# Delta rule: powers, weight casts and value scaling placed elsewhere in ScalarE's queue, the weight subtraction placed later, one output transpose in another PSUM bank

## The chip, the core and the metric

The kernel runs on one core of a Trainium2 chip. The core has five engines that work side by side, each through its own queue in order: TensorE (PE, matrix products; PEld is its weight load), VectorE (DVE), ScalarE (ACT), GpSimd (POOL) and SyncE (SP), which issues most of the DMA transfers. They wait for one another through semaphores. Working data lies in the on-chip memory SBUF; matrix products land in PSUM, which has eight banks. The metric is the device time of one execution in microseconds, lower is better.

## The reference

One inference step of a two-layer encoder over 2048 prompt tokens and 32 sample tokens. The first layer is a gated delta rule with 8 heads of width 128, the second a sliding-window attention. The part that matters here:

```python
def step(s, xs):
    qd, kd, ui, wi, ai, gl = xs
    v_new = ui - jnp.einsum('bhck,bhkv->bhcv', wi, s)
    o = jnp.einsum('bhck,bhkv->bhcv', qd, s) + jnp.einsum('bhij,bhjv->bhiv', ai, v_new)
    s = s * gl[..., None, None] + jnp.einsum('bhck,bhcv->bhkv', kd, v_new)
    return s, o
```

with, for each chunk, decays `exp(gcum_i - gcum_j)`, powers `exp(gcum)`, a unit lower triangular inverse, and afterwards

```python
o = o * lax.rsqrt(jnp.mean(o * o, -1, keepdims=True) + RMS_EPS) * norm_w * jax.nn.silu(z)
out = o.reshape(b, l, A_VW) @ w_out
```

The gate `z` is a slice of `x @ w_in`; the kernel forms such products from a high and a low part of each operand, so a weight is first cast to its high part (`w_hi`), and the low part (`w_lo`) is the weight less that.

## The kernel before

The program has three stages. First come the projections with the short convolution. Then comes the delta stage, which this change touches: `Delta.run` goes over 17 chunks (one of the 32 sample tokens, 16 of 128 prompt tokens). Last come the output projection and the second layer. In the delta stage the orders of TensorE, VectorE and ScalarE are those in which the code emits their instructions, written out by hand; GpSimd's and the DMA queue's orders are the scheduler's.

Each pass of the loop works on several chunks at once: `ch` (chunk i) is finished, `nx` (i+1) gets its errors and the last part of its inverse, `n2` (i+2) is prepared, `n3` (i+3) gets loads and decays. A step is a generator, and `go(...)` runs each generator named up to its next `yield`. The steps, with their lines before the change:

- `lower` (L538): products k·k (`g`), times the decays `E` on VectorE (`npr`, L550), copies to `nb` on ScalarE (L554), a transposition to `L` on VectorE (L559).
- `chain` (L562): the inverse of 32-row blocks, `tm` and `Tt` (L572, L575). For `n2` its first 25 columns run on GpSimd over nearly a whole pass, the rest on VectorE in the next pass.
- `spread` (L638): two VectorE transpositions `tcp` (L645, L646), then ScalarE spreads them (L651). `invert` (L653): products `bps` (L669, L675, L682, L688, L693) with ScalarE copies between them; the last (L694) writes `u`, which `changes` needs.
- `changes` (L707): products `vp` of `u` and `vn` (L714), copied to `vs` by ScalarE (L716). `seen` (L720): the output products `op` (L728, L732). `advance` (L737): products `sp` (L744) and the new state on VectorE (L750). `errors` (L697): products `ks` (L703), subtracted from `vn` (L704).
- `turn_k` (L578): transposes k and scales it on ScalarE to `kd`. `turn_v` (L592): transposes v (`vtr`, L599) and scales it to `vn`: the first four heads in one VectorE operation (L601), the last four in four ScalarE operations (L604).
- `powers` (L623): two ScalarE exponentials of `gb`, in place (L627). `fade` (L630): k and q times `gb` on VectorE (L635). `decays` (L524): one VectorE operation and eight ScalarE exponentials for `E` (L534).
- `squares`, `norms`, `scale`: the output's root mean square, on ScalarE (L760) and VectorE (L767, L423 to L434, L776). `emit` (L779): four transposes of the output into a PSUM tile (`otr`, L786), times z on VectorE (L787), stored.

PSUM: pool `pa` (tag `tr`) and pool `pc` (tag `sc`) have two banks each, `pb` and `pd` one. `vp`, `otr`, `sp` and `ks` take turns in `pc`; the 64-wide products of `invert` alternate between `pb` and `pa`.

Up to pass 10 `fill(us)` puts gate products of the first layer between the steps (`late_z`, L274; `project` with L77 to L79). Their weights are fetched ahead into `w_raw`, cast by ScalarE (L53) and subtracted by VectorE (L54), both in `split`, which `side(False)` calls in the middle of a pass, after the squares. Such a cast falls on every second pass. In the last passes, and afterwards, output products take the filler's place (L1076 to L1078).

Of the kernel before, what the change touches and what calls it, by code (L numbers as in the profile page):

```python
# [10 lines left out]
F32 = mybir.dt.float32  # L11
F32R = mybir.dt.float32r
I32 = mybir.dt.int32
AF = mybir.ActivationFunctionType
ALU = mybir.AluOpType
# [80 lines left out]
class P1:  # L96
# [166 lines left out]
    def split(self):  # L263
        if self.fetched is not None:
            self.next = split_fetched(self.nc, self.wp, self.fetched, self.sub)
            self.fetched = None

# [182 lines left out]
class Delta:  # L450
# [141 lines left out]
    def turn_v(self, ch):  # L592
        nc, G, n = self.nc, self.G, ch.n
        ch.vn = []
        for q in range(2):
            vn = self.four.tile([128, 4, 128], F32, tag="vn", name="vn")
            tr = self.pa.tile([128, 4, 128], F32, tag="tr", name="vtr")
            for j in range(4):
                nc.tensor.transpose(tr[:n, j, :], ch.v[q][:, j, :n], G["ident"][:, :])  # L599
            if q == 0:  # L600
                nc.vector.tensor_tensor(out=vn[:n], in0=tr[:n], in1=self.bc(G["hn"][:n, ch.ti, 0:4], n), op=ALU.mult)  # L601
            else:
                for j in range(4):
                    nc.scalar.activation(vn[:n, j, :], tr[:n, j, :], AF.Copy, scale=G["hn"][:n, ch.ti, 4 + j:5 + j])  # L604
            ch.vn.append(vn)
# [173 lines left out]
    def emit(self, ch):  # L779

        nc, V, T, n = self.nc, self.nc.vector, self.T, ch.n
        for q in range(2):
            z = ch.z[q]
            tr = self.pc.tile([128, 4, 128], F32, tag="sc", name="otr")
            for j in range(4):
# [5 lines left out]
    def run(self, chunks, S, first, second, side, done):  # L791
# [44 lines left out]
        for i in range(len(chunks) + 1):  # L836
# [32 lines left out]
            go(a, t, a, t, seen, sq)  # L869
            side(False)  # L870
            fill(2 * more + gate)
# [10 lines left out]
            if i == 0:  # L882
# [4 lines left out]
                (self.norms, ch), (self.scale, ch)))  # L887
            go(e, t, t)
            drain(t)
            if nx:  # L890
                self.spread(nx)
            go(w, e)
            if n3:
# [3 lines left out]
            d = gen(self.decays, n3)  # L897
            p = gen(self.powers, n2)
            go(v)
            fill(gate)  # L900
            go(r, r, r, g, r, r, v, r, k, r, d)
            if i > self.OPEN:
# [8 lines left out]
            seen = gen(self.seen, nx)  # L911
            go(w, r, p, r, seen, k, r, d, r)
            if n3:
# [7 lines left out]
            fill(more)  # L921
            go(v, o, d)
            if i + 3 == len(chunks):
# [673 lines left out]
def program(tc, I, O, T, G):  # L1597
# [32 lines left out]
    def side(o):  # L1630
        if o is None:
            left.close()
            o1.append(O1(tc, left, I, O, T, G))
        elif o1 and o:
            next(o1[0].on.rest, None)
            if o1[0].steps == 8:
                o1[0].on.tabs = o1[0].on.tables()
            o1[0].steps += 1
        elif not o1 and not o:
            p1.split()  # L1640

    def outputs():
# [207 lines left out]
```

## Time and profile before

| | us |
|---|---|
| median of 3 runs | 2244.25 |
| lowest and highest | 2241.93 and 2248.31 |
| profiled execution | 2235.55 |
| span of the profiled execution | 2233.8 |

| share of the span | busy us | share |
|---|---|---|
| TensorE | 2161.8 | 97% |
| its weight loads | 1982.5 | 89% |
| VectorE | 1378.5 | 62% |
| ScalarE | 900.5 | 40% |
| GpSimd | 838.1 | 38% |

The profile describes one execution. A row of a timeline gives start, length, engine, line, operation, output and inputs, and in brackets how long the engine stood idle before it and which instruction released it. A row of waits gives the waiting engine and instruction, what it waited for, the total, the number of times and the longest. Lengths of matrix products include a tail in which the result drains while the next group already runs, so the distance of starts says more than the length. The share of a whole span is an average over stages: what an edit of one stage is worth is read in that stage.

### The profile page before, as it was taken

What the parts mean: (1) busy time and instruction counts of PE and PEld (TensorE: products, weight loads), DVE (VectorE), ACT (ScalarE), POOL (GpSimd) and SP (SyncE); (2) the same over time, 40 slices, a digit from 0 to 9 for tenths busy, and PEclk for the clock granted to TensorE, in tenths of its full rate; (3) what the DMA queues carried; (4) which work ended last, traced back from release to release, by engine and by line L of the source; (5) the groups of instructions that cost most, each with busy time, mean ns of one, the idle gap of its engine ahead of it and who ended that gap; (6) DMA issues with size and microseconds to landing.
All of it is one profiled execution on the core that took longest, in us unless ns stands there. A gap on an engine that the chain in (4) does not pass through costs nothing.

```text
span 2233.8 us, 36601 instructions
## 1 busy us (share of the span) xinstructions
PE 2161.8 (97%) x13706; PEld 1982.5 (89%) x13706; DVE 1378.5 (62%) x2713; ACT 900.5 (40%) x2235; POOL 838.1 (38%) x1189
## 2 busy tenths in 40 slices
PE   8999999999999999999989999999999999999997
PEld 6999999999999888898878788999999977778885
DVE  3676666753476687878867886135442235668774
ACT  4344444433333566667742212222112235445541
POOL 1422122221211477777731201046441214556563
PEclk9999999999999999999999999999999999999999
DMA  5222122333445244345526764365222277233311
GB/s 195 67 64 82 60 75 66 111 104 110 125 121 162 93 132 126 122 127 188 189 103 202 224 200 141 111 219 175 73 75 69 84 178 249 76 95 96 111 59 57
DMA packets 250529, 274.47 MB, mean 123 GB/s; under 512 B 76096, under 2 KB 195200, under 8 KB 250080
## 3 DMA queue, kind: packets, MB, share of 16 engines
q1 hardware_dynamic: 238352, 248.84, 36.3%
q10 hardware_dynamic: 12000, 23.30, 3.0%
q8 instruction: 108, 1.77, 0.3%
q14 instruction: 69, 0.57, 0.1%
HBM read 168.53 MB, written 103.92 MB: 122 GB/s over the span
## 4 chain that ended last, share of the span: by engine, by line
PE 83%; ACT 7%; DVE 4%; DMA 3%; POOL 1%; issue 1%; ACTq 0%; DVEq 0%; SPq 0%; POOLq 0%
PE ps L77 16%; PE ps L79 16%; PE ps L78 16%; PE po L1076 5%; PE po L1078 4%; PE po L1077 4%; PE ot L1567 4%; PE S L1546 2%; PE tr L1561 2%; PE vp L714 1%; DMA act_raw<-s_hT 1%; ACT kd L588 1%; PE op L732 1%; PE sp L744 1%; PE gq L618 1%
## 5 line engine op out<-in xcount | busy, mean ns | idle before, releaser
L77 PE MATMUL ps<-act_hi,w_hi 128*128 128x416 f32 x2000 | 707.0, 354 | 6.4 <-ACT w_hi L53 5.1
L79 PE MATMUL ps<-act_hi,w_lo 128*128 128x416 f32 x2000 | 704.9, 353 | 1.8 <-POOL w_lo L54 1.2
L78 PE MATMUL ps<-act_lo,w_hi 128*128 128x416 f32 x2000 | 701.6, 351 | 0.5 <-DVE act_lo L69 0.4
L77 PEld LDWEIGHTS ps<-act_hi,w_hi 128*128 128x128 f32 x2000 | 376.8, 189 | 11.9 <-ACT w_hi L53 6.1
L79 PEld LDWEIGHTS ps<-act_hi,w_lo 128*128 128x128 f32 x2000 | 376.1, 188 | 6.7 <-POOL w_lo L54 1.7
L78 PEld LDWEIGHTS ps<-act_lo,w_hi 128*128 128x128 f32 x2000 | 376.4, 188 | 5.4 <-DVE act_lo L69 1.1
L54 POOL TENSOR_TENSOR w_lo<-w_raw,w_hi 128x1024 fp32r<-128x1024 f32 x51 | 135.4, 2655 | 555.7 <-ACT w_hi L53 501.5
L196 DVE SCALAR_TENSOR_TENSOR y<-R,convw,y 128x2083 f32<-128x2083 f32 x72 | 173.7, 2414 | 109.7 <-ACT y L194 74.1
L572 POOL TENSOR_TENSOR tm<-L,Tt 128x60 f32<-128x60 f32 (+19 forms) x373 | 141.1, 378 | 119.6 <-DVE tm L572 47.5
L1554 POOL TENSOR_TENSOR P<-P,sm 128x384 f32<-128x384 f32 (+2 forms) x128 | 100.5, 807 | 181.7 <-DVE sm L1433 106.6
L575 POOL TENSOR_TENSOR Tt<-Tt,tm 128x60 f32<-128x60 f32 (+19 forms) x373 | 152.9, 410 | 29.2
L1429 ACT ACTIVATE P<-S,nm 128x192 f32<-128x192 f32 (+2 forms) x260 | 104.6, 418 | 93.3 <-DVE nm L1422 40.4
L227 ACT COPY R<-ps 128x416 f32<-128x416 f32 (+1 forms) x144 | 61.3, 449 | 199.0 <-PE ps L79 174.7
L53 ACT CAST w_hi<-w_raw 128x1024 fp32r<-128x1024 f32 x62 | 64.9, 1047 | 128.8 <-PE ps L78 99.4
L1076 PE MATMUL po<-wo_hi,g_hi 128*128 128x512 f32 x256 | 103.8, 406 | 1.8 <-ACT hT L1183 1.8
L1273 POOL TENSOR_TENSOR rs<-rs,sin 128x416 f32<-128x416 f32 x50 | 71.1, 1421 | 78.8 <-DVE rs L1272 72.1
L1078 PE MATMUL po<-wo_hi,g_lo 128*128 128x512 f32 x256 | 100.6, 393 | 0.0
L1567 PE MATMUL ot<-pt,vd 128*128 128x256 f32 x372 | 98.7, 392 | 1.9 <-ACT pt L1563 1.5
L1077 PE MATMUL po<-wo_lo,g_hi 128*128 128x512 f32 x256 | 100.3, 392 | 0.0
L1076 PE MATMUL po<-wo,g_hi 128*128 128x512 f32 x240 | 99.3, 414 | 0.0
L1078 PE MATMUL po<-wo,g_lo 128*128 128x512 f32 x240 | 96.2, 401 | 0.0
L1077 PE MATMUL po<-wo,g_hi 128*128 128x512 f32 x240 | 96.1, 400 | 0.0
(304 smaller groups left out, 3984.3 us busy)
## 6 DMA issues: line engine op xcount, KB each, us to landing
w_raw<-in_w_in SPq DMA_DIRECT2D x40, 512.0 KB
w_raw<-in_b_w_in SPq DMA_DIRECT2D x20, 512.0 KB
gb<-s_gcum SPq DMA_DIRECT2D x17, 512.0 KB
k<-s_k SPq DMA_DIRECT2D x17, 512.0 KB
s_bz<-za SPq DMA_DIRECT2D x40, 208.0 KB
s_bq<-ra SPq DMA_DIRECT2D x40, 208.0 KB
s_q<-y SPq DMA_DIRECT2D x8, 1024.0 KB
s_k<-y SPq DMA_DIRECT2D x8, 1024.0 KB
```

What stands on the lines that cost most here:

```text
L54: sub.tensor_tensor(out=lo[:], in0=raw[:], in1=hi[:], op=ALU.subtract)
L77: nc.tensor.matmul(ps, hi[:, k, :], xh[:, k, :], start=(k == 0), stop=False)
L78: nc.tensor.matmul(ps, hi[:, k, :], xl[:, k, :], start=False, stop=False)
L79: nc.tensor.matmul(ps, lo[:, k, :], xh[:, k, :], start=False, stop=(k == KC - 1))
L196: nc.vector.scalar_tensor_tensor(out=y[:], in0=R[:, j:j + W], scalar=self.convw[:, i, j:j + 1], in1=y[:], op0=ALU.mult, op1=ALU.add)
L572: P.tensor_tensor(out=tm[:n, i0 - k:, :w], in0=L[:n, i0:, j:j + 1].to_broadcast(sh), in1=Tt[:n, j:j + 1, :w].to_broadcast(sh), op=ALU.mult)
L575: P.tensor_tensor(out=Tt[:n, i0:, :w], in0=Tt[:n, i0:, :w], in1=tm[:n, i0 - k:, :w], op=ALU.subtract)
L1076: nc.tensor.matmul(ps[:n], ghi[:, k, :n], w[0][:, k, cs], start=a, stop=False)
L1077: nc.tensor.matmul(ps[:n], ghi[:, k, :n], w[1][:, k, cs], start=False, stop=False)
L1078: nc.tensor.matmul(ps[:n], glo[:, k, :n], w[0][:, k, cs], start=False, stop=z)
L1429: nc.scalar.activation(P[u], src, AF.Exp, bias=nm[:, u:u + 1], scale=1.0, accum_out=sm[:, u:u + 1])
L1567: nc.tensor.matmul(ot[:, p], self.vd[:, kc0 + j, p, :], pt[:, 2 * j:2 * j + 2, :], start=(j == 0), stop=(j == nj - 1))
```

## The change

- `split` becomes two steps, `cast` (ScalarE) and `subtract` (VectorE). In the loop `cast` is called where `split` was, behind the new place of the powers, and `subtract` at the end of the pass.
- The powers of `n2` are emitted in the middle of the pass, right behind the squares, and no longer between the parts of `invert`.
- `turn_v` scales all eight heads on ScalarE; its first half is emitted before `spread`.
- The first four exponentials of `E` are emitted behind the last part of `invert` and no longer before it, together with the second four.
- The second half of `inside` comes ahead of three small steps of `norms`.
- `emit` puts the transposes of the first four heads into the bank of `pb`, those of the last four stay in `pc`.

The same instructions run on TensorE and GpSimd in the same order as before.

```diff
     def split(self):
-        if self.fetched is not None:
-            self.next = split_fetched(self.nc, self.wp, self.fetched, self.sub)
-            self.fetched = None
+        self.cast()
+        self.subtract()
+
+    def subtract(self):
+        if isinstance(self.fetched, tuple):
+            raw, hi, lo = self.fetched
+            self.sub.tensor_tensor(out=lo[:], in0=raw[:], in1=hi[:], op=ALU.subtract)
+            self.next, self.fetched = (hi, lo), None
+
+    def cast(self):
+        raw = self.fetched
+        if raw is not None and not isinstance(raw, tuple):
+            hi = self.wp.tile([128, KC, 128], F32R, tag="w_hi", name="w_hi")
+            lo = self.wp.tile([128, KC, 128], F32R, tag="w_lo", name="w_lo")
+            self.nc.scalar.copy(hi[:], raw[:])
+            self.fetched = raw, hi, lo
...
-            if q == 0:
-                nc.vector.tensor_tensor(out=vn[:n], in0=tr[:n], in1=self.bc(G["hn"][:n, ch.ti, 0:4], n), op=ALU.mult)
-            else:
-                for j in range(4):
-                    nc.scalar.activation(vn[:n, j, :], tr[:n, j, :], AF.Copy, scale=G["hn"][:n, ch.ti, 4 + j:5 + j])
+            for j in range(4):
+                h = q * 4 + j
+                nc.scalar.activation(vn[:n, j, :], tr[:n, j, :], AF.Copy, scale=G["hn"][:n, ch.ti, h:h + 1])
...
-            tr = self.pc.tile([128, 4, 128], F32, tag="sc", name="otr")
+            tr = (self.pb.tile([128, 4, 128], F32, tag="tr", name="otr") if q == 0 else
+                  self.pc.tile([128, 4, 128], F32, tag="sc", name="otr"))
...
             go(a, t, a, t, seen, sq)
-            side(False)
+            go(gen(self.powers, n2))
+            side(0)
             fill(2 * more + gate)
...
-            go(e, t, t)
+            go(e, t, t, w)
             drain(t)
             if nx:
                 self.spread(nx)
-            go(w, e)
+            go(e)
             if n3:
                 self.load(n3, "k")
             go(g)
             fill(2 * more + 2 * gate)
             d = gen(self.decays, n3)
-            p = gen(self.powers, n2)
             go(v)
             fill(gate)
-            go(r, r, r, g, r, r, v, r, k, r, d)
+            go(r, g, r, r, r, r, v, r, k, r, d)
...
-            go(w, r, p, r, seen, k, r, d, r)
+            go(w, r, r, seen, k, r, r)
...
-            go(v, o, d)
+            go(v, o, d, d)
+            side(1)
...
-        elif o1 and o:
+        elif o1 and o is True:
...
-        elif not o1 and not o:
+        elif not o1 and o is False:
             p1.split()
+        elif not o1 and o == 0:
+            p1.cast()
+        elif not o1 and o == 1:
+            p1.subtract()
```

## The prediction

> **What bounds the kernel now.** First the whole span, then stretches of it, then passes of the chunk loop. Columns of the stretches: length, then busy time and instruction count of TensorE, its weight loads, VectorE, ScalarE and GpSimd, granted clock, DMA share, GB/s.
>
> ```profile
> span 2233.8 us, 36601 instructions
> ...
> 735.00:1180.00 445.00, 415.57 (x4280) 382.75 (x4279) 341.82 (x825) 291.48 (x903) 294.06 (x746) 0.97 0.43 137
> 1180.00:1300.00 120.00, 117.15 (x562) 96.36 (x561) 102.33 (x242) 25.56 (x31) 21.55 (x10) 1.00 0.71 218
> ...
> 818.14:846.10 27.96, 25.88 (x272) 24.08 (x272) 22.39 (x53) 19.01 (x59) 20.53 (x51) 1.00 0.44 140
> 846.10:872.65 26.55, 25.71 (x272) 24.07 (x272) 21.13 (x52) 18.02 (x58) 18.91 (x49) 1.00 0.41 128
> ...
> 740.00:745.00 5.00, 5.00 (x19) 3.86 (x18) 1.92 (x8) 1.98 (x11) 3.88 (x14) 0.50 0.35 105
> ```
>
> The change touches only the delta stage, 735 to 1180. TensorE stands still there for 445.00 − 415.57 = 29.4 us; after it TensorE is busy 117.15 of 120, so a gain is carried on to the end. I number passes by i, each from the first vp product (L714) to the next. Pass 3 (818.14) has a weight cast, pass 4 (846.10) has none; both carry gate products as filling. From pass 11 on there is no such filling. The waits of the stage (total, times, longest):
>
> ```profile
> DVE k L635 <- ACT gb L627: 21.4, 14, 2.6
> ...
> PE vp L714 <- ACT u L694: 8.3, 15, 1.9
> ...
> PE bps L669 <- DVE tcp L645: 6.0, 9, 1.1
> ...
> PE tr L585 <- ACT ta L677: 3.6, 5, 0.7
> ...
> PE otr L786 <- ACT vs L716: 3.5, 15, 0.2
> ```
>
> TensorE's waits come once a pass: vp for u, the output transposes for vs, and in cast passes L669 and L585. Now pass 4 on TensorE and ScalarE (start, length, idle before in brackets):
>
> ```profile
> 847.99 0.60 PE L786 MATMUL otr<-ident,o 128*128 128x128 f32 x4
> 848.83 0.66 PE L786 MATMUL otr<-ident,o 128*128 128x128 f32 x4 [0.23 <-ACT vs L716]
> ...
> 855.82 0.60 PE L599 MATMUL vtr<-ident,v 128*128 128x128 f32 x4
> 856.25 1.06 PE L703 MATMUL ks<-Sp,k 128*128 128x128 f32 x8
> 857.15 1.06 PE L618 MATMUL gq<-q,k 128*128 128x128 f32 x8
> ...
> 869.73 1.16 PE L549 MATMUL g<-k 128*128 128x128 f32 x8
> 871.04 1.16 PE L549 MATMUL g<-k 128*128 128x128 f32 x8 [0.15 <-ACT kd L588]
> 872.65 1.16 PE L714 MATMUL vp<-vn,u 128*128 128x128 f32 x8 [0.45 <-ACT u L694]
> ...
> 859.50 0.91 ACT L651 ACTIVATE u<-tcp,sides 128x256 f32<-128x256 f32 x2 [3.61 <-DVE tcp L646]
> ...
> 867.78 1.14 ACT L604 ACTIVATE vn<-vtr,t_hn 128x128 f32<-128x128 f32 x4
> 868.80 1.17 ACT L627 ACTIVATE gb<-gb 128x512 f32<-128x512 f32 x2
> 869.84 1.15 ACT L588 ACTIVATE kd<-tr,t_ekd 128x128 f32<-128x128 f32 x4
> 870.84 1.31 ACT L534 ACTIVATE E<-E,t_ngc 128x128 f32<-128x128 f32 x4
> 872.00 0.60 ACT L694 ACTIVATE u<-bps 64x512 f32<-64x512 f32 x1
> 872.48 1.29 ACT L534 ACTIVATE E<-E,t_ngc 128x128 f32<-128x128 f32 x4
> ```
>
> ScalarE is idle 3.61 us in the middle of the pass, but from 867.78 it works without a break up to u, and TensorE waits for the end of that run.
>
> **The change part by part.** TensorE's and GpSimd's instruction orders stay the same. VectorE loses one operation a chunk and has two moved, ScalarE gains four a chunk, and on the DMA queue a weight fetch slips behind four loads; it is fetched more than a pass ahead of its cast, and only if that were gone would the cast wait for it. The two chunks ahead of the loop get the same scaling under gate products: nothing.
>
> **Powers and E (hand-over to the next pass).** The two gb exponentials (from 868.80 to 869.84, 1.04 us) and the first four E exponentials (870.84 to 872.00, 1.16) no longer stand ahead of u. Then kd can end near 869.9 and u near 870.4, and TensorE is its own limit. How much that gives TensorE: uninterrupted, a group of eight takes 857.15 − 856.25 = 0.90, so vp would start 1.80 after the first g instead of 872.65 − 869.73 = 2.92. That is 1.12 a pass; 0.60 of it is shown as idle, 0.52 is the drain of two groups that the profile counts as busy. I take 1.12, the low end being 0.60. What is late next: all eight E exponentials now stand between u and vs. They end about 870.4 + 2.3 = 872.7; vp would start at 871.5 and its first half takes 1.16, so vs is wanted at 872.7: level. The cost lies between 0 and the second four, 1.15 a pass; I take 0.1.
>
> In pass 14 there is no E, and the wait is longer:
>
> ```profile
> 1132.42 2.05 PE L714 MATMUL vp<-vn,u 128*128 128x128 f32 x16 [1.95 <-ACT u L694]
> ```
>
> There only the powers' 1.04 goes: 1.0.
>
> **Other bank for the output transposes.** The second group of otr starts 0.84 after the first; uninterrupted, four transposes take 856.25 − 855.82 = 0.43. Gain 0.41 (0.23 if only the idle counts) in passes 2 to 16; nothing is emitted in passes 0 and 1. The new bank was last read for u, which vp has waited for already, so no wait is added. Without filling VectorE carries the path, and there I take 0.3, the earlier second product with z.
>
> **Value scaling on ScalarE and the late subtraction.** Rows of pass 3 behind those of pass 4:
>
> ```profile
> 859.39 0.65 DVE L601 TENSOR_TENSOR vn<-vtr,t_hn 128x512 f32<-128x512 f32 x1
> ...
> 870.00 1.23 DVE L635 TENSOR_TENSOR k<-k,gb 128x1024 f32<-128x1024 f32 x1 [1.79 <-ACT gb L627]
> ...
> 827.83 1.03 ACT L53 CAST w_hi<-w_raw 128x1024 fp32r<-128x1024 f32 x1
> ...
> 828.89 1.22 DVE L54 TENSOR_TENSOR w_lo<-w_raw,w_hi 128x1024 fp32r<-128x1024 f32 x1 [1.39 <-ACT w_hi L53]
> ...
> 833.03 0.69 PE L669 MATMUL bps<-tcp,npr 32*32 32x32 f32 x32 [0.51 <-DVE tcp L645]
> ...
> 837.77 0.66 PE L585 MATMUL tr<-ident,k 128*128 128x128 f32 x4 [0.72 <-ACT ta L677]
> ```
>
> In a cast pass VectorE stops 1.39 us for the cast and then subtracts for 1.22, ahead of the chain that TensorE needs at L669. Moved to the end of the pass, the subtraction falls into the 1.79 us in which VectorE waited for gb, a wait that goes too; w_lo is not read before the next pass. So a cast pass should cost what pass 4 costs: 27.96 − 26.55 = 1.41, in four passes (1, 3, 5, 7); low end 0. ScalarE must fit its new work ahead of L651. In pass 3 its squares end 827.83 − 818.14 = 9.7 into the pass, with the earlier transposes 9.3; gb 1.04, cast 1.0 and four scalings 1.1 end at 12.4. L651 waits for tcp until 859.50 − 846.10 = 13.4, less 0.4: 13.0. It fits by 0.6 in cast passes, by 1.6 elsewhere; were it not to fit, L675 would wait by the excess, at most the scaling's 1.1.
>
> A scaling of four heads takes 1.14 on ScalarE (L604) against 0.65 on VectorE (L601). [...] The rows agree that each becomes dearer; the sum differs only if ScalarE's middle is on the path, which is a rival below.
>
> **GpSimd's chain.** It is the next thing in the way:
>
> ```profile
> 852.89 0.26 POOL L572 TENSOR_TENSOR tm<-L,Tt 128x31 f32<-128x31 f32 x1 [3.90 <-DVE tm L572]
> ...
> 879.44 0.26 POOL L572 TENSOR_TENSOR tm<-L,Tt 128x31 f32<-128x31 f32 x1 [3.49 <-DVE tm L572]
> ...
> 1040.43 0.26 POOL L572 TENSOR_TENSOR tm<-L,Tt 128x31 f32<-128x31 f32 x1 [1.93 <-DVE tm L572]
> ...
> 1064.31 0.26 POOL L572 TENSOR_TENSOR tm<-L,Tt 128x31 f32<-128x31 f32 x1 [0.46 <-DVE tm L572]
> ...
> 1088.68 0.20 DVE L572 TENSOR_TENSOR tm<-L,Tt 128x42 f32<-128x42 f32 x1 [0.49 <-POOL Tt L575]
> ```
>
> Its idle time before each chain is what a pass can lose before the chain sets the pace. In the filled passes 3.5 to 3.9 are there and 1.5 to 2.9 are wanted: enough. In passes 10 to 12 only 1.93 + 0.46, less 0.2 for the hand-overs, 2.2 in all, against 3 × 1.4 wanted; at 1088.68 VectorE already waits for it.
>
> **The sum**: pass 0: 1.1. Pass 1: 1.1 + 1.4 = 2.5. Passes 2, 4, 6, 8, 9: 5 × (1.12 + 0.41) = 7.7. Passes 3, 5, 7: 3 × (1.53 + 1.41) = 8.8. Passes 10 to 12: 2.2. Pass 13: 1.4. Pass 14: 1.3. Passes 15 and 16: 0.8. Together 25.8, less 0.1 for the E block in 14 passes and a little for cast passes that only just fit: 24. The profiled execution took 2235.55 (span 2233.8 and 1.75 around it): 2211.5. The median of the runs is 2244.25, 8.7 above it, so on that scale **2220**.
>
> **The rivals.**
> 1. Only the idle time returns, the drains stay: 0.60 for 1.12 and 0.23 for 0.41. Then 0.6 + 2.0 + 5 × 0.83 + 3 × 2.24 + 2.2 + 0.8 + 1.2 + 0.5 = 18: 2226. For it: the profile calls drains busy. Against: the groups' starts, 0.90 apart where nothing waits.
> 2. The waits of passes 10 to 13 gather at one place, behind GpSimd's chain, and TensorE's clock falls. The row at 740 shows granted clock 0.50 for a whole 5 us; such a dip costs at least half of it, 2.5. Two more: 2225; one of those now present gone: 2217. [...]
> 3. Slower: the E block decides. If u does not come at least 1.15 earlier against TensorE, vs waits for the second four E exponentials, and the otr, op and sp products behind it: 14 × 1.15 = 16 lost, hand-over and bank gains gone, only the cast's 5.6 kept: 2244 + 16 − 5.6 = 2255. Against: 2.2 us leave ScalarE's run ahead of u and nothing enters it.
> 4. Slower by a little: ScalarE's middle is on the path after all, and each chunk pays 1.14 − 0.65 = 0.49, 17 × 0.49 = 8: 2252. [...] Against: 3.61 idle.
> 5. No effect: what is gained is waited for again behind the stage: 2244. Against: 117.15 of 120 busy there; for it, DMA share 0.71.
>
> **How the numbers follow.** Forecast 0.58 (2220, alone 2212 to 2228), rival 1 0.14, rival 2 0.11, rival 3 0.06, rival 4 0.03, rival 5 0.08. 0.3% is 6.7 us, about the spread of the three runs; the border of faster is 2237.5. Faster 0.58 + 0.14 + 0.11 = 0.83, same 0.08, slower 0.09. Range 2208 to 2236: below the forecast by what a vanished dip and the two ends of the hand-over allow, above it past rivals 1 and 2; what it leaves out is rivals 3 to 5, 0.17.
>
> **What would show it.** Right: vp waits for u under 0.1, second otr 0.43 behind the first, cast passes within 0.3 of the others at about 25.0, VectorE's wait for gb gone, GpSimd's idle before a chain under 0.2 from pass 11 on with VectorE waiting for Tt. Wrong: vs starting over 1.4 after vp (rival 3), L651 without idle before it and L675 waiting for y (rival 4), pass 4 at 25.7 (rival 1), clock below 0.97 in the stage (rival 2), passes shorter but the stretch behind the stage longer (rival 5).

## The result, and the profile after

| | before | after |
|---|---|---|
| median of the timed runs beside each other | 2243.36 us (4 runs) | 2205.64 us (4 runs) |
| lowest and highest | 2241.93 and 2248.31 | 2204.09 and 2207.76 |
| profiled execution | 2235.55 | 2205.77 |
| its span | 2233.8 | 2204.0 |

The changed kernel is faster by 1.7%: its time is 0.9829 of that of the kernel before, with an interval of 0.9811 to 0.9846. In two more sets of runs, each on another chip, the ratio was 0.9846 (0.982 to 0.9872) and 0.9842 (0.9822 to 0.9862). The forecast was 2220 with a range from 2208: the direction was right, the gain larger than said, and the time lies below the range.

The lines of the code have moved by 11 to 13: `vp` is L725 now, `otr` L798, `u` L705, `E` L547, `tcp` L656 and L657, `Sp` L761, the chain L585 and L588. The first line of the page of the changed kernel:

```profile
span 2204.0 us, 36640 instructions
```

The stage and passes 3 and 4 in stretches (columns as in the prediction):

```profile
735.00:1180.00 445.00, 431.22 (x4402) 404.01 (x4401) 358.60 (x872) 311.00 (x968) 296.69 (x747) 0.97 0.47 149
812.15:837.10 24.95, 24.95 (x275) 23.94 (x273) 22.02 (x51) 19.97 (x63) 19.68 (x48) 1.00 0.43 139
837.10:862.05 24.95, 24.95 (x274) 23.94 (x273) 20.90 (x50) 19.01 (x62) 20.12 (x52) 1.00 0.49 155
```

In the same stretch of 445 us, which now holds more of the work, TensorE stands still for 445.00 − 431.22 = 13.8 us in place of 29.4. Pass 3, with a weight cast, and pass 4, without, now take the same 24.95 (27.96 and 26.55 before), and TensorE is busy in all of it. The end of pass 4 on TensorE and on ScalarE:

```profile
860.17 2.05 PE L562 MATMUL g<-k 128*128 128x128 f32 x16
862.05 1.95 PE L725 MATMUL vp<-vn,u 128*128 128x128 f32 x16
863.84 1.04 PE L798 MATMUL otr<-ident,o 128*128 128x128 f32 x8
...
850.21 0.91 ACT L662 ACTIVATE u<-tcp,sides 128x256 f32<-128x256 f32 x2 [1.83 <-DVE tcp L657]
...
860.27 0.59 ACT L705 ACTIVATE u<-bps 64x512 f32<-64x512 f32 x1
860.77 2.43 ACT L547 ACTIVATE E<-E,t_ngc 128x128 f32<-128x128 f32 x8
863.15 0.59 ACT L727 COPY vs<-vp 128x512 f32<-128x512 f32 x1
```

`u` ends at 860.86, 1.19 ahead of the first `vp`; no wait stands in brackets on TensorE. `vp` starts 1.88 after `g` (2.92 before; 1.80 was the forecast). The eight `otr` take 1.04 together and four of them 0.60, so the second four start about 0.44 behind the first. `vs` starts 1.10 after `vp`, straight behind the block of eight `E`. And ScalarE still waits 1.83 for `tcp` in the middle of the pass, with all its new work done. The waits of the stage:

```profile
PE ks L714 <- DVE Sp L761: 6.0, 4, 2.0
DVE tm L585 <- POOL Tt L588: 5.7, 4, 1.7
...
PE bps L680 <- DVE tcp L656: 2.2, 3, 1.2
...
PE vp L725 <- ACT u L705: 0.9, 1, 0.9
```

TensorE's wait for `u` has gone from 8.3 in 15 passes to 0.9 in one (pass 14, with 1.95 before: the 1.0 of the forecast), VectorE's wait for `gb` from 21.4 to nothing. What is late next is seen in the first two rows: in four late passes VectorE waits for GpSimd's `Tt`, the state update `Sp` stands behind that wait in VectorE's queue, and TensorE's `ks` waits for `Sp`, up to 2.0 us.

### The profile page after: what moved, and what is told of

Same layout as the page of the kernel before. It is cut to its first block, busy times and chain, and to the rows that moved or that the text cites. A ratio compares the mean times of both kernels' runs of the same rounds, so it can differ in the third digit from the quotient of the medians.

```text
span 2204.0 us, 36640 instructions
## 1 busy us (share of the span) xinstructions
PE 2152.8 (98%) x13706; PEld 1984.2 (90%) x13706; DVE 1372.1 (62%) x2696; ACT 917.4 (42%) x2303; POOL 843.1 (38%) x1189
## 4 chain that ended last, share of the span: by engine, by line
PE 89%; POOL 3%; DMA 3%; DVE 2%; ACT 2%; issue 1%; ACTq 0%; SPq 0%; DVEq 0%; POOLq 0%
PE ps L77 17%; PE ps L79 17%; PE ps L78 17%; PE po L1089 5%; PE po L1091 5%; PE po L1090 5%; PE ot L1580 4%; PE S L1559 2%; PE tr L1574 2%; POOL Tt L588 1%; POOL tm L585 1%; PE g L562 1%; PE vp L725 1%; PE op L739 1%; PE ks L714 1%
## 5 line engine op out<-in xcount | busy, mean ns | idle before, releaser
L54 POOL TENSOR_TENSOR w_lo<-w_raw,w_hi 128x1024 fp32r<-128x1024 f32 x44 | 117.0, 2660 | 472.3 <-ACT w_hi L53 446.2
L585 POOL TENSOR_TENSOR tm<-L,Tt 128x60 f32<-128x60 f32 (+19 forms) x373 | 139.3, 374 | 89.8 <-PE sp L755 42.9
L588 POOL TENSOR_TENSOR Tt<-Tt,tm 128x60 f32<-128x60 f32 (+19 forms) x373 | 157.2, 421 | 29.2
L53 ACT CAST w_hi<-w_raw 128x1024 fp32r<-128x1024 f32 x48 | 50.3, 1049 | 116.8 <-PE ps L78 88.2
```

What stands on the lines that cost most here:

```text
L54: sub.tensor_tensor(out=lo[:], in0=raw[:], in1=hi[:], op=ALU.subtract)
L585: P.tensor_tensor(out=tm[:n, i0 - k:, :w], in0=L[:n, i0:, j:j + 1].to_broadcast(sh), in1=Tt[:n, j:j + 1, :w].to_broadcast(sh), op=ALU.mult)
L588: P.tensor_tensor(out=Tt[:n, i0:, :w], in0=Tt[:n, i0:, :w], in1=tm[:n, i0 - k:, :w], op=ALU.subtract)
```

## The experiments

Times of the runs in one table; each set has the kernel before beside it on the same chip. "Clock" is the median over the timed runs of the granted clock.

| run | median us | before beside it | ratio, interval | clock |
|---|---|---|---|---|
| before_again | 2238.03 | 2237.03 | 1.0002 (0.9991 to 1.0013) | 0.988 |
| powers_alone | 2230.65 | 2237.03 | 0.9964 (0.995 to 0.9978) | 0.986 |
| bank_alone | 2225.25 | 2237.03 | 0.995 (0.9931 to 0.9969) | 0.992 |
| cast_alone | 2231.98 | 2237.03 | 0.9973 (0.9961 to 0.9986) | 0.989 |
| powers_cast | 2214.11 | 2236.41 | 0.9898 (0.9882 to 0.9915) | 0.992 |
| after_again | 2203.73 | 2238.77 | 0.9846 (0.982 to 0.9872) | 0.991 |
| values_back | 2208.75 | 2238.77 | 0.9864 (0.9836 to 0.9891) | 0.990 |
| e_first | 2206.59 | 2238.77 | 0.9856 (0.9829 to 0.9883) | 0.991 |
| late_split | 2217.3 | 2238.77 | 0.9906 (0.9882 to 0.993) | 0.984 |
| sp_first | 2209.9 | 2236.41 | 0.9876 (0.9861 to 0.989) | 0.987 |
| after_third | 2202.32 | 2239.82 | 0.9842 (0.9822 to 0.9862) | 0.992 |
| warm | 2210.28 | 2239.82 | 0.9866 (0.9842 to 0.9889) | 0.990 |
| before_warm | 2236.68 | 2238.05 | 1.0 (0.9987 to 1.0012) | 0.991 |
| before_third | 2238.28 (one) | 2238.05 | | 0.988 |

Since single executions differ by several us (the runs of the kernel before lie between 2231.5 and 2248.5), the verdicts on a part go by the length of the passes in the traces, which repeat to 0.03 us in passes 1 to 9 of the three profiles of the kernel before. Each part has one profile. The measure is the kernel before in passes 5 (with a cast) and 6 (without):

```profile
872.65:900.57 27.92, 25.85 (x272) 24.07 (x273) 22.20 (x53) 19.01 (x59) 20.49 (x51) 1.00 0.38 122
900.57:927.12 26.55, 25.71 (x272) 24.07 (x272) 21.16 (x52) 18.02 (x58) 18.89 (x49) 1.00 0.41 128
```

### One part at a time

**Powers alone**, on the kernel before:

```diff
+            go(gen(self.powers, n2))
             side(False)
...
-            p = gen(self.powers, n2)
...
-            go(w, r, p, r, seen, k, r, d, r)
+            go(w, r, r, seen, k, r, d, r)
```

> The kernel before with only the powers moved to behind the squares; E, subtraction, value scaling and banks as before. Theory (the hand-over term): u comes 1.04 earlier, TensorE needs 1.12 for its own limit, so 1.0 a pass in passes 0 to 9, 2.2 in all in passes 10 to 12, 1.0 each in passes 13 and 14: 14 us less, 2229 on the scale of a median of 2243.4. If only the idle 0.60 comes back: 6 + 1.8 + 1.2 = 9 less, 2234. If the E exponentials ahead of u are what holds it: under 3 less, 2241.

Passes 5 and 6:

```profile
869.93:897.85 27.92, 25.41 (x274) 24.00 (x272) 22.27 (x53) 19.03 (x59) 21.83 (x55) 1.00 0.37 122
897.85:923.38 25.53, 25.30 (x275) 24.01 (x273) 21.38 (x52) 18.05 (x58) 18.04 (x47) 1.00 0.42 134
```

The subtraction of pass 5 in VectorE's timeline:

```profile
881.73 1.35 DVE L54 TENSOR_TENSOR w_lo<-w_raw,w_hi 128x1024 fp32r<-128x1024 f32 x1 [2.59 <-ACT w_hi L53]
```

Without a cast a pass gains 26.55 − 25.53 = 1.02, the whole of the 1.04 that left ScalarE's run ahead of `u`: the drains come back too, and not only the idle 0.60. In the cast passes the gain is nothing, which was not expected: the powers now stand ahead of the cast, and VectorE waits 2.59 for it ahead of its subtraction. In the kernel before that row was:

```profile
883.41 1.23 DVE L54 TENSOR_TENSOR w_lo<-w_raw,w_hi 128x1024 fp32r<-128x1024 f32 x1 [1.57 <-ACT w_hi L53]
```

So the 1.04 is paid back in the middle of the pass. The median fell by 6.4 where 14 were expected.

**The subtraction alone**, on the kernel before: `side(False)` becomes `side(0)` (cast), and

```diff
             go(v, o, d)
+            side(1)
```

> The kernel before with only the subtraction moved from behind its cast to the end of the pass. Theory: passes 1, 3, 5 and 7 fall from 27.96 to 26.55, 1.41 each: 5.6 less, 2237.8. Rival: the subtraction (1.22) delays the first VectorE products of the next pass: 4 x 0.2, 0.8 less, 2242.6.

Passes 5 and 6:

```profile
870.24:896.80 26.56, 25.71 (x273) 24.08 (x273) 22.49 (x53) 18.97 (x59) 19.36 (x48) 1.00 0.41 128
896.80:923.35 26.55, 25.71 (x273) 24.08 (x273) 21.15 (x52) 18.03 (x58) 19.87 (x52) 1.00 0.41 128
```

Cast passes cost what the others cost, 1.34 to 1.41 less, and nothing is lost in the pass behind: the term held, the rival fell.

**Powers and subtraction together**, the two diffs above on the kernel before:

> The kernel before with the powers moved and the subtraction moved to the end of the pass, the rest as before. Question: powers alone left the cast passes at 27.9 while it took 1.03 from the others, and the subtraction alone took 1.41 from the cast passes; do the two together take the sum? Theory (the powers push the cast back by 1.04, and with it the subtraction that stands ahead of VectorE's chain; once the subtraction is gone from there the cast does not matter): all passes from 2 to 9 at 25.52, cast or not. If the cast itself is now too late for ScalarE's next step: cast passes at 26.0 to 26.6, others at 25.52.

Passes 5 and 6:

```profile
865.27:890.79 25.52, 25.28 (x275) 24.00 (x273) 22.44 (x53) 18.97 (x59) 19.91 (x49) 1.00 0.39 133
890.79:916.31 25.52, 25.28 (x275) 24.02 (x273) 21.12 (x52) 18.04 (x58) 20.32 (x53) 1.00 0.42 134
```

Passes 2 to 9 all take 25.51 or 25.52. The powers need the other edit: they can stand ahead of the cast without loss only because VectorE no longer waits for the cast there.

**The bank alone**, on the kernel before:

```diff
-            tr = self.pc.tile([128, 4, 128], F32, tag="sc", name="otr")
+            tr = (self.pb.tile([128, 4, 128], F32, tag="tr", name="otr") if q == 0 else
+                  self.pc.tile([128, 4, 128], F32, tag="sc", name="otr"))
```

> The kernel before with only the other bank for the first output transposes. Theory: second otr group 0.43 behind the first in place of 0.84; 0.41 a pass in passes 2 to 12 and 0.3 in passes 13 to 16: 5.7 less, 2237.7. Only the idle 0.23 a pass: 3 less, 2240.4. If the next pass's vp waits longer for u by what was gained: no change, 2243.

Pass 6:

```profile
898.77:924.87 26.10, 25.49 (x272) 24.09 (x272) 21.35 (x52) 18.04 (x58) 19.07 (x50) 1.00 0.43 131
```

0.45 a pass (26.55 − 26.10; in pass 5, with a cast, 27.92 − 27.45 = 0.47), for the 0.41 of the forecast, although `vp` still waits for `u` (8.3 in 15 passes, as before): what TensorE gains at one place it doesn't give back at the next. The median fell by 11.8, more than twice the term. In this profile passes 13 and 15 take 24.22 and 29.68; in the first profile of the kernel before they take 27.32 and 33.08, each with a stretch of 6.83 us at half clock, which is missing here. So a good part of the surplus goes with the clock (see below); whether the edit keeps those stretches away was not shown.

**E back ahead of u**, on the changed kernel:

```diff
-            go(w, r, r, seen, k, r, r)
+            go(w, r, r, seen, k, r, d, r)
...
-            go(v, o, d, d)
+            go(v, o, d)
```

> The changed kernel with only the first four E exponentials ahead of u again. Theory: u ends 1.19 ahead of vp in pass 5 of the changed kernel (860.86 against 862.05), the four take 1.16: within 0.1 a pass, same within 2 us. If the E move earned half of the hand-over, 0.5 a pass: 7 slower. If the eight E in one block delay vs (rival 3 of the prediction), this one is faster by up to 0.5 a pass, 7 faster.

Pass 6:

```profile
887.24:912.30 25.06, 25.06 (x274) 24.01 (x272) 20.91 (x51) 19.04 (x62) 20.22 (x53) 1.00 0.43 136
```

25.06 for 24.96, 0.10 a pass: that is the E move's share. Powers 1.02, E 0.10 and bank 0.45 add up to 1.57; the whole change took 26.55 − 24.96 = 1.59 in such a pass. A delay by the block of eight E (rival 3) does not show. The reordering of `inside` was not run alone; 0.02 a pass is left for it and the value scaling together.

**Value scaling back on VectorE**, on the changed kernel:

```diff
-            for j in range(4):
-                h = q * 4 + j
-                nc.scalar.activation(vn[:n, j, :], tr[:n, j, :], AF.Copy, scale=G["hn"][:n, ch.ti, h:h + 1])
+            if q == 0:
+                nc.vector.tensor_tensor(out=vn[:n], in0=tr[:n], in1=self.bc(G["hn"][:n, ch.ti, 0:4], n), op=ALU.mult)
+            else:
+                for j in range(4):
+                    nc.scalar.activation(vn[:n, j, :], tr[:n, j, :], AF.Copy, scale=G["hn"][:n, ch.ti, 4 + j:5 + j])
```

> The changed kernel with only the value scaling undone: the first four heads are scaled by VectorE again, in one operation ahead of the transpositions. Theory (the prediction gave this edit no gain): 0 to 3 slower. Rival: the VectorE operation of 0.65 stands ahead of tcp, for which TensorE's first products of the inverse wait, so 0.3 to 0.65 a pass in 16 passes: 5 to 10 slower.

Passes 1 to 9 take 24.95 and 24.96 as in the changed kernel, so the dearer scaling on ScalarE (1.14 us for four heads against 0.65) costs nothing and brings nothing there; passes 10 to 14 take 118.2 together, against 119.2 in the second and 118.0 in the first profile of the changed kernel. The first `vp` starts at 734.54, against 733.03 and 733.42 in those two profiles, but a window at half clock at 718, which those two lack, has its share in that. The medians differ by 5.0 with intervals that overlap; the trace shows no place for the rest.

### GpSimd's chain and the late passes

**Two more columns for VectorE**, on the changed kernel:

```diff
-    chunks[-1].split = 23
+    for c in chunks[12:]:
+        c.split = 23
```

> The changed kernel with the last four chunks but one handing two more columns of the inverse from GpSimd to VectorE (23 in place of 25). Theory (GpSimd's chain sets the pace from pass 11 on): VectorE's waits for Tt (5.7 in 4 passes) and TensorE's for Sp behind them (6.0) go, VectorE gets 0.8 a pass more, partly inside waits that it has: 2 to 5 faster. If VectorE is the limit there anyway: 2 to 4 slower. If the clock decides these passes: within 2, with the halved stretches at other places.

It is 13.6 slower than the changed kernel beside it. Waits of the late passes (985 to 1145):

```profile
PE bps L680 <- DVE tcp L656: 8.6, 5, 2.4
...
DVE tm L585 <- POOL Tt L588: 1.0, 1, 1.0
...
PE ks L714 <- DVE Sp L761: 0.9, 4, 0.2
```

Pass 12, in which the granted clock fell to 0.82:

```profile
1036.56:1064.55 27.99, 25.35 (x251) 23.78 (x249) 21.42 (x53) 19.90 (x62) 19.69 (x50) 0.82 0.51 170
```

The waits for `Tt` and `Sp` went as expected, and a longer one came: VectorE with two columns more is late with `tcp`, which the `bps` products need. My theory named the wrong owner of these passes; VectorE's sequence up to `tcp` is in the way as well as GpSimd. Passes 11 to 13 take 79.9 together, 70.7 in the second profile of the changed kernel; each of the three holds a stretch of 6.8 or 10.2 us at half clock, so the loss is not VectorE's alone.

**State updates ahead of the chain**, on the changed kernel, from pass 12 on:

```diff
-            go(vp, vp, z, z, x, x, low, low, t)
+            late = i > self.OPEN
+            go(vp, vp, z, z, x, x, low, low)
+            if not late:
+                go(t)
...
-            go(seen, a, t, a, t)
+            go(seen, a, a) if late else go(seen, a, t, a, t)
...
-            go(a, t, a, t, seen, sq)
+            go(a, a, t, t, t, t, t, t, t, seen, sq) if late else go(a, t, a, t, seen, sq)
```

> The changed kernel; from pass 12 on VectorE's eight state updates Sp come ahead of its steps of the inverse and no longer between them. Question: what are TensorE's waits for Sp in the late passes (2.05 us each in passes 12 to 14) worth, and do the halved clocks come from them? Theory: VectorE updates Sp in the 1.3 to 1.7 us in which it stood waiting for GpSimd's Tt, ks no longer waits, and tcp comes 1.3 earlier: 1.3 a pass in passes 12 to 14, 4 us; and the halved stretches behind these waits (1043, 1067, 1091 in the two profiles) go too, 1.7 each, up to 5 more: 4 to 9 faster than the changed kernel, granted clock of its runs 0.993. If GpSimd's chain alone sets the pace of these passes: nothing in the passes beyond the dips, 0 to 2. If the halved clocks have nothing to do with the waits, they stay in passes 12 to 14.

Waits of the late passes, then two windows of pass 13:

```profile
PE bps L680 <- DVE tcp L656: 6.2, 4, 1.8
...
PE ks L714 <- DVE Sp L761: 0.2, 1, 0.2
```

```profile
1066.34:1069.75 3.41, 1.65 (x42) 1.46 (x41) 3.17 (x11) 1.80 (x7) 2.71 (x10) 1.00 0.99 371
1069.75:1073.17 3.42, 3.42 (x33) 3.13 (x27) 2.23 (x7) 1.62 (x4) 2.79 (x9) 0.50 0.65 250
```

Again the wait moved, from `ks` to `bps`, and it now stands ahead of the products of the inverse. TensorE is busy 1.65 of the 3.41 us of the first window, and in the next the clock is halved; the run is not faster (ratio 0.9876), where 4 to 9 us were expected. Neither kernel beats the changed one.

### Why single executions differ: the granted clock

**The two kernels once more.**

> The kernel before, unchanged, run and profiled once more. Question: why its first profiled execution (2235.55 us) was 8 us under its timed runs (median 2243.36), while the changed kernel's profiled execution equals its median. Theory: one execution differs from the next by several us, in places outside the delta stage (a weight transfer that lands late, a clock dip), and the first profiled one was a short one. Then the new profiled execution lies between 2238 and 2248, the distances of the first vp products of the passes are again 26.55 (no cast) and 27.96 (cast) within 0.15, and the extra time shows as waits behind the stage. Rival: being profiled makes this kernel shorter by about 8: then the new profiled execution is again 2234 to 2237 while the median of the timed runs is 2243.

> The changed kernel, unchanged, run and profiled once more beside the kernel before on this chip. Question: does the part of the gain that the prediction's sum did not hold come from single executions or from the mechanism? Theory: the passes repeat (24.95 in passes 1 to 9 within 0.05), the differences between executions lie in the passes from 10 on, where the granted clock halves at different places; the ratio to the kernel before, with its median over many runs (2237 in the last set), is 0.985 to 0.988, a gain of 27 to 33 and not of 38. Rival: the gain is a steady 38 (ratio 0.983), and the sum of the prediction lacks some 12 us of mechanism in the passes.

> The changed kernel a third time, as the measure for the run with the added products on the same chip. Passes 1 to 9 at 24.95; passes 12 to 14 at 24.37 where the clock halves behind the wait of 2.05 and at 23.7 where it does not; median 2203 to 2207, ratio to the kernel before 0.983 to 0.988.

> A third profile of the kernel before, unchanged. Theory: passes 0 to 10 as in the other two within 0.1, except pass 0; passes 11, 13 and 15 either 23.9, 24.2 and 30 without a halved stretch or 2.8 to 5.5 longer with one, and the time of the execution follows their sum. Rival: the execution is longer or shorter by several us with the same halved stretches.

The new profiled executions of the kernel before took 2236.55 and 2238.28, next to medians of 2238.03 and 2238.05, so a profile does not shorten it. The theory had the wrong place for what differs: not behind the stage, but in passes 11 and 15 (26.65 against 23.87, 35.59 against 33.08 in the first profile). Its 79 timed runs in these sets go with their granted clock: 14 with 0.990 or more have a median of 2234.3, 38 with 0.988 or 0.989 one of 2237.0, 19 with 0.986 or 0.987 one of 2241.2, 8 below that 2241.6. The first profiled execution had 0.990 and 2235.55. The 13 runs of the changed kernel have a median of 2204.1, with clocks of 0.989 to 0.994.

The gain expected of the second set, 27 to 33, was missed as well: beside each other the medians differ by 37.7, 35.0 and 37.5 in the three sets. In the last two of them the clock is 0.986 in the kernel before and 0.991 and 0.992 in the changed one, while in the other sets the kernel before has 0.988 or 0.989 and medians of 2236.4 to 2238.1. By the medians above, runs with 0.986 or 0.987 are some 7 us longer than runs with 0.990 or more. So part of the gain seems to be time at half clock that the kernel before has and the changed one has not, and its size differs from set to set.

Where the clock goes is seen in pass 11 of the first profile of the kernel before, then in the same pass of the second profile with three windows of it:

```profile
1033.64:1057.51 23.87, 21.61 (x249) 19.80 (x249) 19.70 (x50) 17.63 (x57) 18.42 (x47) 1.00 0.71 234
```

```profile
1032.26:1058.91 26.65, 24.55 (x249) 22.51 (x249) 19.79 (x50) 17.75 (x57) 20.60 (x54) 0.87 0.58 206
...
1042.45:1045.86 3.41, 2.04 (x44) 1.74 (x43) 3.17 (x10) 0.86 (x2) 2.77 (x9) 1.00 0.87 270
1045.86:1049.28 3.42, 3.42 (x25) 3.08 (x24) 3.01 (x11) 0.80 (x3) 2.73 (x9) 0.50 0.49 187
1049.28:1052.69 3.41, 3.41 (x47) 3.08 (x47) 2.97 (x7) 2.08 (x6) 3.10 (x5) 0.50 0.00 0
```

The same pass of the same program takes 23.87 or 26.65. In the longer one TensorE stands still 1.37 in the window from 1042.45 (waits for `tcp` and `vn`), and the next two windows run at half clock. The same happened in pass 13 of all three profiles of the kernel before (27.2 to 27.5), and in pass 11 of two.

The changed kernel has such a window behind its 2.05 wait for `Sp`. Pass 13 and its windows in the first profile, then in the second:

```profile
1057.07:1080.78 23.71, 20.86 (x250) 19.69 (x249) 20.83 (x49) 19.68 (x62) 19.81 (x50) 1.00 0.60 202
...
1063.87:1067.28 3.41, 1.75 (x16) 1.56 (x15) 2.66 (x13) 3.33 (x12) 2.64 (x10) 1.00 0.94 285
1067.28:1070.70 3.42, 2.27 (x26) 2.06 (x25) 3.15 (x12) 1.20 (x5) 2.72 (x10) 1.00 1.04 394
```

```profile
1057.51:1081.88 24.37, 22.32 (x250) 21.31 (x249) 20.61 (x49) 19.69 (x62) 20.46 (x51) 0.93 0.62 207
...
1063.90:1067.32 3.42, 1.37 (x13) 1.18 (x12) 1.87 (x9) 3.34 (x12) 2.64 (x11) 1.00 0.90 273
1067.32:1070.73 3.41, 3.41 (x19) 3.41 (x18) 3.00 (x13) 1.60 (x5) 2.72 (x9) 0.50 0.92 350
```

With 1.66 still in one window nothing followed; with 2.05 the next window was halved. It cost only 24.37 − 23.71 = 0.66, not half of 3.41: in the execution without it TensorE stands still for another 3.42 − 2.27 = 1.15 in that next window, waiting for `tcp`, and in the halved one it does not.

**The wait filled with work**, on the changed kernel:

```diff
+            if i > self.OPEN and n2:
+                warm = self.pb.tile([128, 4, 128], F32, tag="tr", name="warm")
+                for j in range(12):
+                    self.nc.tensor.transpose(warm[:, j % 4, :], self.G["ident"][:, :], self.G["ident"][:, :])
             go(e, t, t, w)
```

> The changed kernel with twelve transpositions of the identity added on TensorE in each of passes 12 to 14, into a PSUM tile that nobody reads, at the place where it waits 2.05 for Sp. They take 12 x 0.107 = 1.3 of the wait and compute nothing that is used. Question: is it the standing still that halves the clock there? Theory: TensorE then stands still 0.8 in place of 2.05, no halved stretch begins at 1043, 1067 or 1091, passes 12 to 14 take 23.7 in every execution, and the runs are 0 to 3 us shorter than those of the changed kernel beside it. Rival: the halving goes by the program's place, not by the wait: the halved stretches stay, passes at 24.37. Second rival: the added products delay ks or the bps products: passes above 24.4.

TensorE in pass 12, then the window that was halved in the changed kernel:

```profile
1039.66 1.47 PE L904 MATMUL warm<-ident 128*128 128x128 f32 x12
1041.88 1.16 PE L714 MATMUL ks<-Sp,k 128*128 128x128 f32 x8 [0.75 <-DVE Sp L761]
...
1046.55 0.69 PE L680 MATMUL bps<-tcp,npr 32*32 32x32 f32 x32 [1.24 <-DVE tcp L656]
```

```profile
1042.77:1046.19 3.42, 2.54 (x23) 2.33 (x21) 3.18 (x12) 1.17 (x5) 2.71 (x10) 1.00 1.04 407
```

The wait for `Sp` shrank to 0.75 and all three halved windows are gone, as expected if they come from the standing still. One profile doesn't prove it: in passes 12 to 14 of the runs with values back on VectorE and with E ahead of `u` no window is halved either, without any added products; there no window holds more than 1.73 of standing still. But the passes did not become shorter than without a halved window (24.12, 24.12 and 23.84): TensorE, at full clock, now waits 1.24 for `tcp`. The median was 8 above that of the changed kernel beside it; its profile has the difference behind the loop (1074.7 from the last `vp` to the end, 1064.2 in the third profile of the changed kernel), not in these passes: there TensorE has 29.2 us at half clock against 22.1, and stands still for 35.0 against 28.0. No cause was found that ties it to the edit.

**The same in the kernel before**:

```diff
+            if i >= 10 and n2:
+                warm = self.pb.tile([128, 4, 128], F32, tag="tr", name="warm")
+                for j in range(8):
+                    self.nc.tensor.transpose(warm[:, j % 4, :], self.G["ident"][:, :], self.G["ident"][:, :])
             go(v)
             fill(gate)
```

> The kernel before with eight transpositions of the identity added on TensorE in each of passes 10 to 14, into a PSUM tile that nobody reads, where it waits 0.86 to 1.15 for tcp; they compute nothing that is used. Question: is the surplus of the median of the kernel before over its profiled execution time at half clock, set off by such waits? Theory: the halved stretches of 6.8 in passes 11 and 13 (1046 and 1097 in the second profile) go, those passes take 23.9 and 24.3 in place of 26.65 and 27.2, the mean granted clock of the runs rises from 0.988 to at least 0.990, and the median is 3 to 6 us under that of the kernel before beside it, though TensorE does more work. Rival: the surplus has another cause (transfers, the chip): median and clock within 1 us and 0.001. Second rival: the added products delay the bps products: 5 passes by up to 0.9, 1 to 4 us slower.

Passes 11 and 13:

```profile
1033.79:1057.69 23.90, 22.49 (x256) 20.66 (x256) 19.83 (x50) 17.64 (x57) 17.42 (x45) 1.00 0.61 216
...
1081.75:1106.70 24.95, 22.59 (x256) 20.69 (x257) 21.59 (x51) 18.63 (x58) 20.90 (x52) 1.00 0.52 192
```

Passes 11 and 13 run at full clock and take 23.90 and 24.95, and the clock of the runs (12 beside 17) rises from 0.988 to 0.991, as expected; the median, however, falls by 1.4 where 3 to 6 were expected, and the ratio is 1.0.

The widest evidence is all sixteen profiles, from 20 us on, each cut into the windows of 3.41 us of its own grid. Of the windows at full clock, 67 had TensorE standing still for 1.85 or more, and a halved window followed every one. Between 1.15 and 1.85 it followed 41 of 112. Below 1.15 it followed 16 of 9893, one in each profile, all at the head of the loop (last section). So in these profiles every halved stretch away from that place begins behind a window in which TensorE stood still for 1.15 or more. The stretches are one part of what makes one execution longer than another, but a kernel rid of some of them need not be shorter by their sum. What the rest of the spread is stays open.

## Why the prediction was wrong, and where it was right

**The step that failed** is the last one: "The median of the runs is 2244.25, 8.7 above it, so on that scale 2220". Against the changed kernel's own profiled execution (2205.77) the sum came out at 2211.5, 5.7 too high; the other 8.7 of the 14.4 are that distance. I took it for a constant that belongs to the measurement and that the changed kernel would have too. It was the difference between one execution at a granted clock of 0.990 and three runs of a kernel whose runs lie anywhere from 2231.5 to 2248.5; the median of the 79 later ones is 2237.7, 6.5 below that of the three. The changed kernel's profiled execution lies 0.1 from its median: nothing of the 8.7 is there. How much of the 8.7 was the chance of three runs, and how much time at half clock that the change takes away, the runs do not separate. With the 8.7 taken off forecast and range, the time would have been inside the range. So it would with the 5.7 taken off instead: the miss is the sum of both, and the 8.7 is the larger part.

**The remaining 5.7.** The span fell by 29.8, the forecast was 24. The terms, on the two first profiles and on the mean of the three profiles of each kernel:

| passes | forecast | first profiles | mean of three |
|---|---|---|---|
| 0 | 1.1 | 1.11 | 0.62 |
| 1 to 9 | 19.0 | 19.46 | 19.49 |
| 10 to 12 | 2.2 | 3.09 | 4.84 |
| 13 | 1.4 | 3.61 | 3.41 |
| 14 | 1.3 | −0.50 | −0.65 |
| 15 and behind | 0.8 | 2.2 | 3.8 |
| ahead of the loop | 0 | 0.8 | 0.8 |
| margins taken off | −1.8 | 0 | 0 |
| sum | 24 | 29.8 | 32.3 |

On the mean the sum lacks 8.3 and not 5.7. The difference lies in passes 10 to 12, where two of the three profiles of the kernel before have a halved stretch in pass 11, and from pass 15 on.

- Hand-over (1.12): right, 1.02 for the powers and 0.10 for E, shown by the runs with one part each. The 1.04 of the powers comes back whole, which rival 1 denied.
- Other bank (0.41): right, 0.45.
- Cast passes (1.41): right, 1.34 to 1.41. Not foreseen was that the powers need this edit: without it they earn nothing in a cast pass. The slack of 0.6 in ScalarE's middle held: in pass 3, with a cast, ScalarE still waits 0.83 for `tcp` (at 825.21 in the first profile of the changed kernel).
- Value scaling (nothing): right in passes 1 to 9, but most likely not ahead of the loop, where the prediction put it at nothing because it lies under gate products. In the first profile of the kernel before, TensorE's second transposition of the values waits there for VectorE's scaling; in that of the changed kernel it doesn't:

```profile
723.35 0.66 PE L599 MATMUL vtr<-ident,v 128*128 128x128 f32 x4 [0.56 <-DVE vn L601]
```

```profile
722.60 0.60 PE L612 MATMUL vtr<-ident,v 128*128 128x128 f32 x4
```

The first transposition starts at 720.63 and 720.60, so the second comes 2.72 and 2.00 behind it: 0.7 of the 0.8. The seven profiles with all scaling on ScalarE reach the first `vp` at 732.7 to 733.4, the nine others at 733.7 to 734.8. The run with the scaling back on VectorE does not settle it, because of its halved window at 718.

- The 0.1 for the block of E, and the margin for cast passes, had no cause; 1.8 of the 5.7.
- Passes 10 to 12: the wait for `Tt` came as forecast, in four passes, 1.7 at most, and from 1017.14 to 1125 no row of GpSimd has idle time before it; 0.9 more was gained than I had allowed.
- Passes 13 and 14 were mis-sized by the clock: the kernel before lost 2.4 to 2.7 to halved windows in pass 13 (27.32; without them 24.95 with the added transpositions, and 24.22 with the bank alone, 0.4 of that the bank's own), which the change freed, and the changed kernel lost 0.5 in pass 14 to the one behind its 2.05 wait for `Sp` (24.07; 23.56 without one in the run with E ahead of u). Rival 2 had the clock fall where the waits gather, with the sign both ways, at an estimate of 2.5 for one dip, half of the 5 us of its row at 740; no row of the prediction ties the clock to the waits, the count over sixteen profiles above does. It was held less likely than the forecast (0.11).
- Behind the stage TensorE waits for weight casts. In the first profile of the kernel before and of the changed kernel:

```profile
PE ps L77 <- ACT w_hi L53: 4.1, 1, 4.1
...
ACT w_hi L53 <- DMA w_raw<-in_b_w_in: 3.9, 1, 3.9
```

```profile
ACT w_hi L53 <- DMA w_raw<-in_b_w_in: 2.2, 2, 1.9
...
PE ps L77 <- ACT w_hi L53: 1.5, 2, 1.0
```

In all 4.1 − 1.5 = 2.6 that no term held. The three profiles of the kernel before have 3.1 to 4.1 here and those of the changed kernel 1.4 to 2.0, but the run with E ahead of u has 3.5, the changed kernel with the added transpositions 4.0, and the kernel before with them 2.0, so it is no property of the change that the runs could pin down; why the weight lands earlier stays open. Rival 5, that the gain is waited for again behind the stage, had the wrong sign.

## What to carry to other kernels

Work out a gain on the trace's own scale and give the time there; a distance between the profiled execution and a median of three runs is no constant of the program (8.7 in the kernel before, 0.1 in the changed one), least of all where it can be the difference of two granted clocks (medians of 2234.3 at 0.990 or more and 2241.2 at 0.986 or 0.987). Move work together: an edit that is worth 1.02 in one pass was worth nothing in the next kind of pass until a second edit took the consumer out of its way. Where an engine's wait is lifted in a stage with three engines close to one another, ask which of them has the next deadline: here the same 2 us went from `ks` to `bps` in two runs, and neither gained.

## What the hardware showed that was not expected

- TensorE's granted clock was 0.50 in stretches of 3.41, 6.83 or 10.24 us, but for the one that the end of the program cuts off, on a grid of 3.41 us: in the first profile of the kernel before, stretches begin at 738.25, 1096.65 and 1154.68, 105 and 17 steps of 3.413 apart. The grid's offset differed between executions: a window begins at 1039.98 in the first profile of the changed kernel, at 1039.36 with the added transpositions and at 1041.00 with two more columns for VectorE. The halved stretches of the rows above begin at the end of a window in which TensorE stood still for only a part: 1.37 of 3.41 with 6.83 at half clock behind it, 2.05 with 3.41 behind it, and 1.76 in pass 13 of the run with the state updates ahead of the chain, where the clock of the pass was 0.87. 1.66 passed without one, so below the 1.85 of the count above the idle time alone does not decide; what else does stays open.
- Whether a halved window followed the same wait went, in two cases, with where the grid cut it. With values back on VectorE, the wait of 2.05 for `Sp` in pass 14 (1089.84 to 1091.89) was cut at 1090.33 into 0.49 and 1.56, and no halved window followed; in the second profile of the changed kernel 2.03 of the same wait lay in one window, and the next was halved. In pass 11 of the kernel before (23.87 or 26.65), the waits for `tcp` and `vn` put 1.37 into one window in the second profile, and 0.53 and 0.83 into two windows in the first.
- How long a halved stretch lasted went with the products at its start. Between 900 and 1180 us the sixteen profiles have 39 stretches. In 27 of them the first halved window holds 64x64 products, as behind the wait for `tcp`, and all of these last 6.8 or 10.2 us. In the other 12 it holds none, as behind the changed kernel's wait for `Sp`, and 11 of them last 3.41, one 6.8. In the two first profiles, the first window of the stretch of 6.83 from 1096.65 in the kernel before holds 64x64 products, and the stretch of 3.41 from 1043.39 in the changed kernel holds products of 128x128 alone. This fits the prices above: 2.4 to 2.7 for the stretch of 6.8 in pass 13 of the kernel before, 0.5 to 0.7 for those of 3.41 in the changed one.
- At the head of the loop, near 737, there is a halved stretch of 6.8 to 10.2 us in all sixteen profiles, with at most 0.27 us of idle time in the 3.41 ahead of it (10.24 from 738.25 in the first profile of the kernel before, 10.24 from 736.19 in that of the changed kernel). There TensorE begins with the small products of the chunk of 32 tokens (the first `vp` at 733.03 is 32*32 in the changed kernel's timeline). What halves the clock there was not shown.
